# Two of x's row tiles on ScalarE's DMA queue and the remainder columns of w as fp32 on SyncE's, in a seven-product QKV projection

## The chip, the cores and the metric

The kernel runs on one core of one Trainium2 chip. The metric is the device time of one execution in microseconds (us). The engines are called as the profile calls them: PE is TensorE (PEld its weight loads), DVE is VectorE, ACT is ScalarE, POOL is GpSimd, SP is SyncE, which only issues DMAs here. ACTq and SPq are the DMA-issuing sides of ACT and SP.

## The reference

```python
batch, seq, hidden = 16, 512, 768
qkv = np.matmul(x, w_qkv)            # x: (16, 512, 768) fp32, w_qkv: (768, 2304) fp32
q, k, v = qkv[..., :768], qkv[..., 768:1536], qkv[..., 1536:]
return np.stack([q, k, v], axis=0).astype(np.float32)
```

So it is one matrix product of 8192 x 768 by 768 x 2304, whose columns are stored as three outputs.

## The kernel before, in words

**Tiling.** x's 8192 rows are 32 *pairs* of two 128-row tiles (`p` is a pair, `r` the tile in it). K = 768 is KT = 6 slices of 128, in two halves of KH = 3. w's 2304 columns are two column groups of 1024 (`q` = 0, 1, each two blocks `c` of CB = 512) and a remainder of REM = 256 columns between them (columns 1024 to 1279). A pair times a column group is a 2 x 2 by 2 x 2 block product, which `quad` and `do` (lines 233 to 289) make from seven products of three matmuls each instead of eight: products 1 and 2 use x and w rounded to bf16 (`xb`, `b1`), products 3 to 7 use sums of blocks of x (`sums_x`, line 211) and of w (`sum_w`, line 112; t1 to t4) and w's block `b22`. The remainder columns are plain bf16 matmuls of x's rounded tile with `w_rem` (`rem_row`, line 304, from `rem`; `rems_by_halves`, line 328). All matmuls of the seven products carry line 251, all those of `block` line 487, the remainder's lines 306 and 334.

**The first pairs.** At the start w is not there yet, so the first ND = 2 pairs (four row tiles) go another way. Their rows are loaded as they lie (`load_row`), cast to bf16 half by DVE and half by ACT (`cast_row`, lines 172 and 173), turned by PE against an identity (`turn_row`, line 190) and copied out of PSUM, and their products with the four 512-column blocks are plain bf16 matmuls in `block` (line 487), which takes the slices of w one after the other, in the order in which they land and are cast (`cast_j`, lines 463 and 465). Between the turns PE runs dummy matmuls on zeros (`busy`, line 458). From the third pair on, x is loaded in parts, turned by DVE (`transpose`, line 154), rounded by ACT or POOL (`round_row`, line 207, `round_x`) and summed.

**The order.** The schedule is written out by hand (`manual_schedule`): each engine runs its instructions in the order in which the program names them, and each DMA queue in the order of its issues. Eight completion semaphores are used in turn for the DMAs of SP and ACT, so that an issue waits for the landing of the eighth DMA before it. The start up to the third pair is in lines 428 to 590:

- SP issues the first row tile; ACT issues two *touches* (lines 431 and 432), 128 x 32 elements of w and of x that nobody reads, and then runs a tiny activation (line 433); SP issues the other three row tiles.
- SP issues 13 slices of w: column group 0, c = 0 (the first of its six K slices in two halves, `lo` and `hi`) and c = 1; then the third pair's rows in eight parts (`load_x_rows(2)`), then two blocks of column group 1 (`load_blocks(1, 0)`).
- POOL issues the remainder columns of w in two K halves, as DMAs that cast fp32 to bf16 (line 450). Two *holds*, one-element copies on POOL (line 445), keep these DMAs back until the last slice of c = 0 has landed, and later POOL work until the first part of the third pair's rows has.
- PE: eight dummies, the four tiles' turns with dummies between, `block(0, 0)` (27 matmuls, the first six of 256 columns), `block(0, 1)` (24), the remainder of the first two pairs by K halves (24, line 334), products 1 and 2 of the third pair (6), the third pair's remainder (12), and then the third pair's other products woven into `block(1, 0)`.
- ACT, behind `block(0, 1)`: the evacuations of tiles 0 and 1 (`late`, line 477), the rounding of the third pair's first tile, the first pair's remainder copy (line 323), tiles 2 and 3, the rounding of the second tile, the second remainder copy, the evacuation of product 1 (line 260).
- DVE: casts of w's slices, t1, one cast, t2, the third pair's two transposes, then its sums and t3, t4.

From the fourth pair on, `two`, `group` and `last` run the steady state.

Of the kernel before, what the change touches and what calls it, by code (L numbers as in the profile page):

```python
# [10 lines left out]
def kernel(  # L11
# [20 lines left out]
    nc = tc.nc  # L32
    P = 128
    G = 32
# [4 lines left out]
    KT = K // P  # L39
    KH = KT // 2  # L40
    KC = K // 4
    NP = M // (2 * P)
    CB = 512
    REM = N3 - 4 * CB
    Q_OFF = (0, 2 * CB + REM)
    R_OFF = 2 * CB
    fp32 = mybir.dt.float32
# [3 lines left out]
    add = mybir.AluOpType.add  # L51
    sub = mybir.AluOpType.subtract

    x_flat = x.rearrange("b t h -> (b t) h")
# [7 lines left out]
    o_pool = ctx.enter_context(tc.tile_pool(name="o", bufs=5))  # L62
# [7 lines left out]
    m_pool = ctx.enter_context(tc.tile_pool(name="m", bufs=2))  # L70
    ps_pool = ctx.enter_context(tc.tile_pool(name="ps", bufs=8, space=bass.MemoryType.PSUM))
# [5 lines left out]
    w_rem = [w_pool.tile([P, KH, REM], bf16, name="w_rem0"), None]  # L77
# [13 lines left out]
    def load_w(dst, j0, nj, off, cols):  # L91
        rows = w_qkv.rearrange("(p j) n -> p j n", j=KT)
        nc.sync.dma_start(dst, rows[:, j0:j0 + nj, off:off + cols])

    stage = {}

    def load_slices(c, cuts):
        t = tq_pool.tile([P, KT, CB], fp32, name="st0", tag="tq")
        stage[0, 0, c], stage[0, 1, c] = t[:, :KH, :], t[:, KH:, :]
        for j, nj, lo, hi in cuts:  # L100
            load_w(t[:, j:j + nj, lo:hi], j, nj, Q_OFF[0] + c * CB + lo, hi - lo)
# [10 lines left out]
    def sum_w(q, n):  # L112
        t1, t2, t3, t4 = ts[q]
        o, in0, in1 = {
            1: (t1, stage[q, 0, 1], stage[q, 0, 0]),
            2: (t2, stage[q, 1, 1], t1),
            3: (t3, stage[q, 1, 1], stage[q, 0, 1]),
            4: (t4, stage[q, 1, 0], t2),
        }[n]
        nc.vector.tensor_tensor(o, in0, in1, op=sub)  # L120

    xin, xf, xb, sr = {}, {}, {}, {}
# [8 lines left out]
    def load_x_rows(p, parts=range(8)):  # L131
        if p not in xin:
            xin[p] = xin_pool.tile([P, 2 * P // G, KC], fp32, name="xin")
        rows = x_flat[p * 2 * P:(p + 1) * 2 * P, :].rearrange("(g b) k -> b g k", b=G)
        for n in parts:
            r, i = divmod(n, 4)
            gs = slice(r * P // G, (r + 1) * P // G)
            nc.sync.dma_start(
                xin[p][i * G:(i + 1) * G, gs], rows[:, gs, i * KC:(i + 1) * KC]
            )  # L140
# [21 lines left out]

    def load_row(p, r):
        if r == 0:
            xin[p] = xin_pool.tile([P, 2, K], fp32, name="xin")
        row = (2 * p + r) * P
        nc.sync.dma_start(xin[p][:, r], x_flat[row:row + P, :])

    def copy_halves(dst, src):
        nc.vector.tensor_copy(out=dst[0], in_=src[0])
# [27 lines left out]
    act, dve = nc.scalar, nc.vector  # L200

    def round_row(p, r, eng):
        n = slice(r * P, (r + 1) * P)
        if r == 0:
            xb[p] = xb_pool.tile([P, KT, 2 * P], bf16, name="xb", tag="xb")
        if eng is act:
            eng.activation(xb[p][:, :, n], xf[p][:, :, n], ident)
        else:
            eng.tensor_copy(out=xb[p][:, :, n], in_=xf[p][:, :, n])
# [23 lines left out]
    def quad(p, q, pool=o_pool, tag="o"):  # L233
        u = Quad()
        u.p, u.q = p, q
        u.o = pool.tile([P, 2, 2 * CB], fp32, name="o", tag=tag)
        u.x = u.y = u.z = None
        return u

    def product(u, n, ps, start):  # L240
        t1, t2, t3, t4 = ts[u.q]
        if n <= 2:
            h = (n - 1) * KH
            lhs = [xb[u.p][:, h + j, :P] for j in range(KH)]
            rhs = [b1[u.q][:, h + j, :] for j in range(KH)]
        else:
            k, t = {3: (4, b22[u.q][:]), 4: (0, t4), 5: (1, t1), 6: (2, t2), 7: (3, t3)}[n]
            lhs = [sr[u.p][:, k, j, :] for j in range(KH)]
            rhs = [t[:, j, :] for j in range(KH)]
        for j in range(KH):  # L250
            nc.tensor.matmul(  # L251
                ps[:], lhs[j], rhs[j],
                start=(start and j == 0), stop=(j == KH - 1), skip_group_check=True,
            )

    def bank():
        return ps_pool.tile([P, CB], fp32, name="ps")

    def evacuate(u):
        nc.scalar.activation(u.o[:, 0, :CB], u.x[:], ident)  # L260

    def do(u, n, out=True):
        c11, c12 = u.o[:, 0, :CB], u.o[:, 0, CB:]
        c21, c22 = u.o[:, 1, :CB], u.o[:, 1, CB:]
        if n == 1:
            u.x = bank()
            product(u, 1, u.x, True)
            if out:
                evacuate(u)
        elif n == 2:  # L270
            u.z = bank()
            product(u, 2, u.z, True)
            nc.vector.tensor_tensor(c11, c11, u.z[:], op=add)  # L273
        elif n == 6:
            product(u, 6, u.x, False)
            nc.scalar.activation(c12, u.x[:], ident)  # L276
        elif n == 5:
            u.y = bank()
            product(u, 5, u.y, True)
        elif n == 7:  # L280
            product(u, 7, u.x, False)
            nc.scalar.activation(c22, u.x[:], ident)  # L282
            nc.vector.tensor_tensor(c22, c22, u.y[:], op=add)  # L283
        elif n == 4:
            product(u, 4, u.x, False)
            nc.scalar.activation(c21, u.x[:], ident)  # L286
        elif n == 3:
            product(u, 3, u.y, False)
            nc.vector.tensor_tensor(c12, c12, u.y[:], op=add)  # L289

    def rows_of(s, p, lo, hi):
        return out_flat[s, p * 2 * P:(p + 1) * 2 * P, lo:hi].rearrange("(r m) n -> m r n", m=P)
# [26 lines left out]
    def rem_copied(p, ps, eng=nc.sync):  # L319

        def copied():
            o = or_pool.tile([P, 2, REM], fp32, name="orem")
            act.activation(o[:], ps[:], ident)  # L323
            return lambda: eng.dma_start(rows_of(1, p, R_OFF - H, R_OFF - H + REM), o[:])

        return copied

    def rems_by_halves(pairs):
        banks = [ps_pool.tile([P, 2, REM], fp32, name="ps") for _ in pairs]
        for h in range(2):  # L330
            for p, ps in zip(pairs, banks):
                for r in range(2):
                    for j in range(KH):
                        nc.tensor.matmul(  # L334
                            ps[:, r, :], xb[p][:, h * KH + j, r * P:(r + 1) * P],
                            w_rem[h][:, j, :], start=(h == 0 and r == 0 and j == 0),
                            stop=(h == 1 and j == KH - 1), skip_group_check=True,
                        )
        return [rem_copied(p, ps) for p, ps in zip(pairs, banks)]

    def two(a, b, early, u=None, turns=()):

# [83 lines left out]
    ND = 2  # L426
    zero = xb_pool.tile([P, CB], bf16, name="zero", tag="xb")
    nc.vector.memset(zero[:], 0.0)
    load_row(0, 0)
    touch = m_pool.tile([P, 2, G], fp32, name="touch")  # L430
    nc.scalar.dma_start(touch[:, 0], w_qkv.rearrange("(p j) n -> p j n", j=KT)[:, 0, :G])  # L431
    nc.scalar.dma_start(touch[:, 1], x_flat[2 * P:3 * P, :G])
    nc.scalar.activation(tiny[:], zero[:, :1], ident)
    make_identity(nc, eye)
    load_row(0, 1)
    load_row(1, 0)
    load_row(1, 1)
    half = CB // 2
    load_slices(0, [(0, 1, 0, half), (0, 1, half, CB)] + [(j, 1, 0, CB) for j in range(1, KT)])
    load_slices(1, [(j, 1, 0, CB) for j in range(KT)])  # L440
    load_x_rows(2)

    def hold(src):
        mark = m_pool.tile([P, 1], fp32, name="mark")
        nc.gpsimd.tensor_copy(out=mark[:], in_=src)

    hold(stage[0, 1, 0][:, KH - 1, :1])
    for h in range(2):
        rows = w_qkv.rearrange("(p j) n -> p j n", j=KT)[:, h * KH:(h + 1) * KH]
        nc.gpsimd.dma_start(w_rem[h][:], rows[:, :, R_OFF:R_OFF + REM])  # L450
    hold(xin[2][:, 0, :1])
    load_blocks(1, 0)

    def busy(n):
# [94 lines left out]
    for f in late0:  # L549
# [3 lines left out]
    cast_j(0, 1, bt, 4, act)  # L553
    cast_j(0, 1, bt, 5, act)
    sum_w(0, 2)
    nc.gpsimd.tensor_copy(out=b22[0][:], in_=stage[0, 1, 1])
    late = block(
        0, 1, bt, [((j, ), range(4)) for j in range(KH)] + [(range(KH, KT), range(4))]
    )
    rems = rems_by_halves(range(2))  # L560
    transpose(2, 2)

    late[0]()
    late[1]()
    round_row(2, 0, act)
    rem_stores = [rems[0]()]
    late[2]()
    late[3]()
    round_row(2, 1, act)
    rem_stores.append(rems[1]())  # L570
    load_blocks(1, 1)
    for store in rem_stores:
        store()
    load_x_rows(3)
    for p in range(2):
        store_quad(quads[p, 0])
# [2 lines left out]
    sums[0](nc.gpsimd)  # L579
    sums[1](dve)  # L580
    sums[2](dve)
    sum_w(0, 3)
    sums[3](dve)
    sums[4](dve)

    u = quad(2, 0)
    do(u, 1)
    do(u, 2)
    cast_j(1, 0, b1[1], 0)
    rem2 = rem(2)  # L590
    middle(u, (5, 6))
# [120 lines left out]
```

## Time and profile before

| what | value |
|---|---|
| runs | 359.88, 359.97, 360.47 us; median 359.97 us |
| the profiled execution | 360.26 us, its span 358.5 us |
| PE / DVE / ACT / POOL busy | 351.8 / 231.7 / 185.5 / 178.5 us |
| DMA | 107.73 MB, 301 GB/s over the span |
| issues at the start | SP's four row tiles from 0.74 us, 13 slices of w from 2.59, the third pair's rows from 11.17, the blocks of column group 1 from 16.98 |
| POOL's two DMAs of the remainder | issued from 12.22 us, 6.7 us from issue to landing (median) |

Times in the profile run from the span's start. A matmul's busy time overlaps the next one's, so the spacing of starts is what counts for PE. A row of the timeline gives start, length, engine, line, operation, output and inputs, how many were merged, and in brackets how long the engine had stood idle before it and what ended the idle time.

### The profile page before, as it was taken

How to read it: one execution, taken by the hardware profiler on the slowest of the kernel's cores; microseconds unless marked ns; L12 is line 12 of the kernel's file. 1: busy time of each engine (PE TensorE's matmuls, PEld its weight loads, DVE VectorE, ACT ScalarE, POOL GpSimd, SP SyncE). 2: the span in 40 equal slices, each digit the busy share in tenths (PEclk: the TensorE clock that was granted, in tenths of full speed). 3: DMA queues.
4: the chain of work that ended last, by engine and by line, in shares of the span. 5: the costliest groups of instructions: out<-in, count | busy, mean ns of one | idle time of the engine just before them, and what ended most of it. 6: DMA issues, size and time to landing. Idle time of an engine off the chain costs nothing.

```text
span 358.5 us, 5212 instructions
## 1 busy us (share of the span) xinstructions
PE 351.8 (98%) x1760; PEld 252.6 (70%) x1780; DVE 231.7 (65%) x245; ACT 185.5 (52%) x316; POOL 178.5 (50%) x187
## 2 busy tenths in 40 slices
PE   8999999999999999999999999999999999999995
PEld 4465577767768687786867768687776867768764
DVE  3789776878475675746676474676647577544643
ACT  5469644445545545454554545545454544545443
POOL 0223775582664717447372664717447371754420
PEclk9999999999999999999999999999999999999999
DMA  7998999999999898989989799898989989755767
GB/s 265 347 373 313 323 353 360 369 346 342 339 298 317 286 261 328 261 317 299 289 323 250 309 283 332 282 264 329 268 293 307 294 321 251 312 217 224 273 243 256
DMA packets 82106, 107.73 MB, mean 301 GB/s; under 512 B 5408, under 2 KB 62240, under 8 KB 82080
## 3 DMA queue, kind: packets, MB, share of 16 engines
q1 hardware_dynamic: 74288, 101.86, 86.1%
q10 hardware_dynamic: 6992, 5.15, 5.9%
q0 software_dynamic: 800, 0.39, 0.8%
q8 instruction: 14, 0.23, 0.3%
q14 instruction: 12, 0.10, 0.1%
HBM read 32.28 MB, written 75.50 MB: 301 GB/s over the span
## 4 chain that ended last, share of the span: by engine, by line
PE 93%; DMA 4%; ACT 1%; ACTq 1%; issue 0%
PE ps L251 78%; PE ps L306 11%; PE ps L487 4%; DMA st<-in_w_qkv_dram 3%; DMA touch<-in_x_dram 1%; PE ps L334 1%; ACT o L286 0%; ACTq L385 0%; ACT orem L399 0%; ACT both L463 0%; ACTq L431 0%; ACTq L401 0%; ACTq L399 0%
## 5 line engine op out<-in xcount | busy, mean ns | idle before, releaser
L251 PE MATMUL ps<-t,s 128*128 128x512 f32 x720 | 178.5, 396 | 0.0
L251 PEld LDWEIGHTS ps<-t,s 128*128 128x128 f32 x720 | 134.9, 188 | 29.8 <-ACT o L276 0.3
L154 DVE STREAM_TRANSPOSE xf<-xin 128x1536 f32<-128x1536 f32 (+1 forms) x33 | 91.2, 2767 | 2.5 <-DMA xin<-in_x_dram 2.5
L218 POOL TENSOR_TENSOR s<-xf 128x384 fp32r<-128x384 f32 x29 | 30.8, 1061 | 116.4 <-PE ps L251 115.0
L251 PE MATMUL ps<-b,xb 128*128 128x512 bf16 x342 | 81.7, 379 | 1.2
L283 DVE TENSOR_TENSOR o<-o,ps 128x512 f32<-128x512 f32 x58 | 39.7, 685 | 60.2 <-ACT o L282 60.2
L251 PEld LDWEIGHTS <-xb 128*128 128x128 bf16 x360 | 33.8, 98 | 36.9 <-issue 4.7
L273 DVE TENSOR_TENSOR o<-o,ps 128x512 f32<-128x512 f32 x60 | 39.0, 681 | 29.5 <-PE ps L251 22.4
L282 ACT ACTIVATE o<-ps 128x512 f32<-128x512 f32 x58 | 34.7, 598 | 44.2 <-PE ps L251 44.2
L276 ACT ACTIVATE o<-ps 128x512 f32<-128x512 f32 x60 | 36.0, 600 | 36.6 <-PE ps L251 34.0
L289 DVE TENSOR_TENSOR o<-o,ps 128x512 f32<-128x512 f32 x60 | 41.1, 687 | 20.7 <-PE ps L251 19.6
L260 ACT ACTIVATE o<-ps 128x512 f32<-128x512 f32 x60 | 35.7, 597 | 31.3 <-PE ps L251 18.3
L251 PE MATMUL ps<-b,s 128*128 128x512 f32 x180 | 50.4, 389 | 0.0
L198 POOL CAST xb<-xf 128x1536 bf16<-128x1536 f32 x28 | 41.0, 1464 | 16.7 <-DVE xf L154 16.7
L286 ACT ACTIVATE o<-ps 128x512 f32<-128x512 f32 x60 | 35.9, 598 | 24.3 <-PE ps L251 21.3
L306 PE MATMUL ps<-w_rem,xb 128*128 128x256 bf16 x360 | 44.6, 273 | 0.0
L306 PEld LDWEIGHTS <-xb 128*128 128x128 bf16 x360 | 34.9, 98 | 11.0 <-issue 1.1
L251 PEld LDWEIGHTS ps<-b,s 128*128 128x128 f32 x180 | 33.8, 188 | 7.1
L219 POOL TENSOR_TENSOR s<-s,xf 128x384 fp32r<-128x384 f32 x29 | 29.3, 1009 | 1.3
L220 POOL TENSOR_TENSOR s<-xf 128x384 fp32r<-128x384 f32 x29 | 29.3, 1009 | 0.0
L222 POOL TENSOR_TENSOR s<-xf,s 128x384 fp32r<-128x384 f32 x29 | 29.3, 1009 | 0.0
L323 ACT ACTIVATE orem<-ps 128x512 f32<-128x512 f32 x31 | 18.5, 597 | 20.7 <-PE ps L306 10.9
(47 smaller groups left out, 127.4 us busy)
## 6 DMA issues: line engine op xcount, KB each, us to landing
out_dram<-o SPq DMA_DIRECT2D x62, 768.0 KB, 4.5
xin<-in_x_dram SPq DMA_DIRECT2D x90, 192.0 KB, 6.5
out_dram<-o SPq DMA_DIRECT2D x65, 256.0 KB, 3.7
out_dram<-orem SPq DMA_DIRECT2D x31, 256.0 KB, 5.5
xin<-in_x_dram ACTq DMA_DIRECT2D x22, 192.0 KB, 6.9
st<-in_w_qkv_dram SPq DMA_DIRECT2D x11, 256.0 KB, 5.2
st<-in_w_qkv_dram SPq DMA_DIRECT2D x3, 768.0 KB, 10.0
xin<-in_x_dram SPq DMA_DIRECT2D x4, 384.0 KB, 4.5
```

What stands on the lines that cost most here:

```text
L154: lambda g=g: nc.vector.transpose(turned[:, g:g + n], rows[:, g:g + n])
L198: nc.gpsimd.tensor_copy(out=xb[p][:], in_=t[:])
L218: 1: lambda g: g.tensor_tensor(s[:, 1], a21, a22, op=add),
L251: nc.tensor.matmul(ps[:], lhs[j], rhs[j], start=(start and j == 0), stop=(j == KH - 1), skip_group_check=True,)
L260: nc.scalar.activation(u.o[:, 0, :CB], u.x[:], ident)
L273: nc.vector.tensor_tensor(c11, c11, u.z[:], op=add)
L276: nc.scalar.activation(c12, u.x[:], ident)
L282: nc.scalar.activation(c22, u.x[:], ident)
L283: nc.vector.tensor_tensor(c22, c22, u.y[:], op=add)
L286: nc.scalar.activation(c21, u.x[:], ident)
L289: nc.vector.tensor_tensor(c12, c12, u.y[:], op=add)
L306: nc.tensor.matmul(ps, xb[p][:, j, r * P:(r + 1) * P], w_rem[j // KH][:, j % KH, :], start=(j == 0), stop=(j == KT - 1), skip_group_check= ...
```

## The change

- The touch of x goes. ACT now issues the touch of w, x's second row tile and its fourth; SP issues the first and the third, and then w's slices.
- The two holds and POOL's two casting DMAs go. SP loads the remainder columns as fp32 into a buffer of the output pool, in two K halves: the first after w's slices, then the first four parts of the third pair's rows, the second half, the other four parts. POOL casts each half to bf16, ahead of its cast of `b22`.
- PE runs the first K half of the first two pairs' remainder (12 matmuls), then products 1 and 2 of the third pair (6), then the second K half (12). On ACT product 1's evacuation stands behind the evacuations of tiles 2 and 3, and both remainder copies behind the rounding of the third pair's second tile. DVE's addition of product 2 stands ahead of t3.

```diff
-    def load_row(p, r):
+    def load_row(p, r, eng=nc.sync):
...
-        nc.sync.dma_start(xin[p][:, r], x_flat[row:row + P, :])
+        eng.dma_start(xin[p][:, r], x_flat[row:row + P, :])
...
-    def rems_by_halves(pairs):
-        banks = [ps_pool.tile([P, 2, REM], fp32, name="ps") for _ in pairs]
-        for h in range(2):
-            for p, ps in zip(pairs, banks):
...
-        return [rem_copied(p, ps) for p, ps in zip(pairs, banks)]
+    def rems_half(pairs, banks, h):
+        for p, ps in zip(pairs, banks):
+            for r in range(2):
+                for j in range(KH):
+                    nc.tensor.matmul(
+                        ps[:, r, :], xb[p][:, h * KH + j, r * P:(r + 1) * P],
+                        w_rem[h][:, j, :], start=(h == 0 and r == 0 and j == 0),
+                        stop=(h == 1 and j == KH - 1), skip_group_check=True,
+                    )
...
-    load_row(0, 0)
-    touch = m_pool.tile([P, 2, G], fp32, name="touch")
-    nc.scalar.dma_start(touch[:, 0], w_qkv.rearrange("(p j) n -> p j n", j=KT)[:, 0, :G])
-    nc.scalar.dma_start(touch[:, 1], x_flat[2 * P:3 * P, :G])
+    touch = m_pool.tile([P, G], fp32, name="touch")
+    nc.scalar.dma_start(touch[:], w_qkv.rearrange("(p j) n -> p j n", j=KT)[:, 0, :G])
+    for p in range(2):
+        load_row(p, 0)
+        load_row(p, 1, nc.scalar)
     nc.scalar.activation(tiny[:], zero[:, :1], ident)
     make_identity(nc, eye)
-    load_row(0, 1)
-    load_row(1, 0)
-    load_row(1, 1)
     half = CB // 2
     load_slices(0, [(0, 1, 0, half), (0, 1, half, CB)] + [(j, 1, 0, CB) for j in range(1, KT)])
     load_slices(1, [(j, 1, 0, CB) for j in range(KT)])
-    load_x_rows(2)
-
-    def hold(src):
-        mark = m_pool.tile([P, 1], fp32, name="mark")
-        nc.gpsimd.tensor_copy(out=mark[:], in_=src)
-
-    hold(stage[0, 1, 0][:, KH - 1, :1])
-    for h in range(2):
-        rows = w_qkv.rearrange("(p j) n -> p j n", j=KT)[:, h * KH:(h + 1) * KH]
-        nc.gpsimd.dma_start(w_rem[h][:], rows[:, :, R_OFF:R_OFF + REM])
-    hold(xin[2][:, 0, :1])
+    st_rem = o_pool.tile([P, KT, REM], fp32, name="str", tag="o")
+    load_w(st_rem[:, :KH], 0, KH, R_OFF, REM)
+    load_x_rows(2, range(4))
+    load_w(st_rem[:, KH:], KH, KH, R_OFF, REM)
+    load_x_rows(2, range(4, 8))
     load_blocks(1, 0)
...
     sum_w(0, 2)
+    for h in range(2):
+        nc.gpsimd.tensor_copy(out=w_rem[h][:], in_=st_rem[:, h * KH:(h + 1) * KH])
     nc.gpsimd.tensor_copy(out=b22[0][:], in_=stage[0, 1, 1])
     late = block(
         0, 1, bt, [((j, ), range(4)) for j in range(KH)] + [(range(KH, KT), range(4))]
     )
-    rems = rems_by_halves(range(2))
+    banks = [ps_pool.tile([P, 2, REM], fp32, name="ps") for _ in range(ND)]
+    rems_half(range(ND), banks, 0)
     transpose(2, 2)
 
     late[0]()
     late[1]()
     round_row(2, 0, act)
-    rem_stores = [rems[0]()]
+    u = quad(2, 0)
+    u.x, u.z = bank(), bank()
+    for n, ps in ((1, u.x), (2, u.z)):
+        product(u, n, ps, True)
+    rems_half(range(ND), banks, 1)
     late[2]()
     late[3]()
+    evacuate(u)
     round_row(2, 1, act)
-    rem_stores.append(rems[1]())
     load_blocks(1, 1)
-    for store in rem_stores:
-        store()
+    for p, ps in enumerate(banks):
+        rem_copied(p, ps)()()
     load_x_rows(3)
...
     sums[2](dve)
+    c11 = u.o[:, 0, :CB]
+    dve.tensor_tensor(c11, c11, u.z[:], op=add)
     sum_w(0, 3)
...
-    u = quad(2, 0)
-    do(u, 1)
-    do(u, 2)
     cast_j(1, 0, b1[1], 0)
```

More of the change, by code (lines that the diff above doesn't have):

```diff
@@ L326, in rem_copied @@
         return copied
-    def rems_by_halves(pairs):
-        banks = [ps_pool.tile([P, 2, REM], fp32, name="ps") for _ in pairs]
-        for h in range(2):
-            for p, ps in zip(pairs, banks):
[L332 to L338, printed above, removed]
-        return [rem_copied(p, ps) for p, ps in zip(pairs, banks)]
+    def rems_half(pairs, banks, h):
[7 more added lines that the diff above has]
+                    )
     def two(a, b, early, u=None, turns=()):
```

## The prediction

> **What bounds the kernel now.** First the page: busy time by engine, then its chain of work.
>
> ```profile
> PE 351.8 (98%) x1760; PEld 252.6 (70%) x1780; DVE 231.7 (65%) x245; ACT 185.5 (52%) x316; POOL 178.5 (50%) x187
> ...
> PE 93%; DMA 4%; ACT 1%; ACTq 1%; issue 0%
> ```
>
> TensorE is busy nearly always, and the chain that ended last is 93% TensorE. So only the rest of the chain can be saved. Where does it lie? The chain in order of time (start, length, what):
>
> ```profile
> 5.23 5.24 DMA st<-in_w_qkv_dram
> 10.48 6.09 DMA st<-in_w_qkv_dram
> 16.60 0.64 ACT both L463
> 17.28 2.32 PE ps L487 x10
> 19.60 2.62 PE ps L334 x24
> ```
>
> From 17.28 us to the last evacuations it is TensorE without a hole worth naming; before that it runs through w's slices. But the chain does not say how long TensorE stood still. `block` (L487) starts at 8.83; its 27 matmuls of q=0, c=0 (start to start 6 of 256 columns take 0.109 each, as the 24 in 2.62 above, and 21 of 512 take 0.2155) make 5.18, and the next 24 begin at 14.03: no stall. These 24 need 5.17, so the remainder (L334) could begin at 19.20; it begins at 19.43 (shown in the last fence below). **The last slice therefore costs 0.23 us**, not the six that its chain piece shows. What else can move is the start at 8.83, and the timeline shows what sets it (start, length, engine, line, operation):
>
> ```profile
> 5.29 1.06 PE L458 MATMUL ps<-zero 128*128 128x512 bf16 x2
> 6.49 0.84 PE L190 MATMUL ps<-eye,xc 128*128 128x128 bf16 x6
> 7.13 0.64 PE L458 MATMUL ps<-zero 128*128 128x512 bf16 x2
> 7.60 0.50 PE L190 MATMUL ps<-eye,xc 128*128 128x128 bf16 x6
> ...
> 8.46 0.54 PE L190 MATMUL ps<-eye,xc 128*128 128x128 bf16 x6
> 8.83 1.03 PE L487 MATMUL ps<-b,xb 128*128 128x256 bf16 x7
> ```
> ```profile
> 6.72 0.52 ACT L173 ACTIVATE xc<-xin 128x384 bf16<-128x384 f32 x1 [0.29 <-DMA xin<-in_x_dram]
> ...
> 7.88 0.52 ACT L173 ACTIVATE xc<-xin 128x384 bf16<-128x384 f32 x1
> ```
>
> x's fourth tile (issued 2.12, landed 5.7 later) is cast at 7.88 and turned at 8.46, and `block` follows. From issue plus time to landing, the four tiles land at 4.04, 5.1, 6.65 and 7.82, and w's first half slice at 2.59 + 5.6 = 8.19, close behind. By windows the DMA moved 124 GB/s in 1.5 to 2.5 us, 297 in 5.5 to 7, 383 in 7 to 8.5 and 402 in 8.5 to 13.5: from 2.5 us on it is full, and bytes decide. Later:
>
> ```profile
> 13.50:15.00 1.50, 1.50 (x9) 0.69 (x7) 1.25 (x3) 1.42 (x3) 0.42 (x1) 1.00 1.05 395
> 15.00:19.00 4.00, 3.93 (x19) 1.66 (x17) 3.23 (x4) 2.98 (x6) 0.26 (x2) 1.00 1.28 248
> ```
>
> (The last two columns are DMA share and GB/s.) While POOL's casting load of the remainder columns runs, the rate falls to 248. Under it the third pair's rows come in:
>
> ```profile
> 18.71 1.60 DVE L154 STREAM_TRANSPOSE xf<-xin 128x768 f32<-128x768 f32 x1 [0.25 <-DMA xin<-in_x_dram]
> 19.43 2.78 PE L334 MATMUL ps<-w_rem,xb 128*128 128x256 bf16 x24
> 20.35 0.84 ACT L207 ACTIVATE xb<-xf 128x768 bf16<-128x768 f32 x1 [1.41 <-DVE xf L154]
> 22.05 1.46 PE L251 MATMUL ps<-b,xb 128*128 128x512 bf16 x5
> ```
>
> Rounded rows are ready at 21.19 and wanted at 22.05, 0.86 of slack, which the change spends: it puts half of the 24 remainder matmuls (12 x 0.109 = 1.31) behind the third pair's first two products. With that order, today's times would bring product 1 at 22.05 - 1.31 = **20.74**. That is the mark I compare with.
>
> **The change part by part.**
>
> *x's tiles on two queues.* SP issues two tiles instead of four, so w's slices are issued some 0.95 earlier (two issues of about 0.43, and gaps); ACT issues touch, tile 2, tile 4. How two queues share the engines is seen in the touches, 16 KB each on ACT's queue: the first took 3.5 us (landed 4.24, beside tile 1 at 4.04), the second 4.0 (5.2, beside tile 2 at 5.1). A queue's packet seems to go in turn with one of the other queue's, as many packets each. Then tile 2 comes only after the touch, that is after tile 1, in turn with tile 3, and tile 4 in turn with w's first half slice. Tile 1 stays at 4.04; tiles 2 and 3 land together near tile 3's old 6.65, or 0.4 sooner if tile 3 follows as closely as tile 2 followed tile 1 (1.1); tile 4 waits for the half slice's 128 KB beside it, 0.34 us at 383 GB/s: 8.16. I take +0.3 for the start of `block`. Bounds: -0.4, if two queues lift 297 to 402 GB/s in 5.5 to 7 us (1.5 x 105/402); +1.5, under the second rival. The value is nearest to the half slice's own landing, 8.19, on which `block` hangs anyway. The Trainium skill, DMA: Bandwidth & Descriptors, section "Queues, rings and completion order", states this turn-taking, packet by packet, and its "Issuing engines are not separate DMA queues" that a second issuing engine only saves issue time; by that alone the start would gain nothing, and the touches' landings agree. ACT's third issue (0.43) delays its table load (1.28, from 1.66) and the tiny activation to about 3.6; the first cast at 4.08 hides it.
>
> *The second touch, the two holds and POOL's loads go.* No engine on the path waited for them. With w's slices alone on the queue the last one needs 4.74 MB moved. Summed over half-microsecond windows before, that is reached at 14.8; with the lag of about 1.0 that the others show it lands at 15.8 instead of 16.6, cast by 16.5. TensorE, started at 9.13, wants it at 9.13 + 5.20 + 14 x 0.2155 = 17.35. So **-0.23**, certain unless the start comes 0.9 earlier.
>
> *The remainder as fp32 between the rows.* SP's queue now holds 0.39 MB of w, four row parts (0.39), 0.39 of w, four parts. At 350 GB/s (between 333 in 19 to 21 us and 395) they land near 16.9, 18.0, 19.1 and 20.3. POOL casts each half: 0.73, half of its 128x1536 cast (1.47), up to the 2.20 that its 128x768 cast took beside VectorE. Ready by 19.1 and 21.3; wanted at 19.50 (9.13 + 5.20 + 5.17) and 19.50 + 2.61 = 22.1: **0**, covered by 0.4 and 0.8; uncovered up to 0.5. POOL's b22 cast (1.47 to 3.02) queues behind them and ends by 24.3; product 3 wants it near 27.7.
>
> *Product 1 earlier.* Rows at 18.0, VectorE free of t2's sum (1.76, from 16.2) at 18.0, transpose 1.60, round 0.84 and two hand-overs: 20.55. TensorE comes at 8.83 + 0.3 + 5.20 + 5.17 + 1.31 = 20.81. **0**; if the rows land at 18.7 as today, 21.2 and +0.4; at 19.2, +0.9.
>
> *Moved behind.* On ACT the evacuation of product 1 comes after the last two tiles' evacuations, near 22.4; VectorE's new addition waits for it and has sums until 23.2: 0. Both remainder copies stand behind round_row, ending near 24.3 (24.39 before); SP's stores wait for them, with eight loads of the fourth pair behind: unchanged. The two blocks of w behind the rows land earlier.
>
> **Sum:** 20.81 - 20.74 = **+0.07 us** (+0.30 - 0.23). From there TensorE's work is the same. The profiled execution took 360.26 (span 358.5, 1.76 around it): 360.33. It lay 0.29 over the median of the runs, 359.97, so I name 360.0.
>
> **The rivals.**
>
> *The start is filled (faster).* The DMA's poor stretches are 1.5 to 2.5 us (124 GB/s) and 5.5 to 7 (297, share 0.89). Two queues could keep the engines fed: against 402 they lost 0.28 and 0.16 MB, 1.1 us. Then TensorE reaches product 1 at 20.81 - 0.30 - 1.1 = 19.41 and the rows are ready at 20.55 - 1.1 = 19.45, so -1.3: 358.7 by the median. Against it: in the first stretch the packets wait though two tiles are already issued. Chance 0.11.
>
> *TensorE starts at half rate (slower).* Its 512-column matmuls start 0.427 apart until about 7.3 (the two at 5.29 take 1.06, the two at 7.13 only 0.64), 0.2155 apart from 9.7. It stands still at 6.15 to 6.49 only, since tile 2 is there at 5.1. If tile 2 lands at 6.65, cast 0.52, turning starts at 7.2: a hole of 1.0. If such a hole keeps the rate low, transposes (0.64), two dummies (0.85), transposes, a dummy (0.43), transposes follow from 7.2: 0.64 + 0.85 + 0.64 + 0.43 + 0.64 = 3.2, `block` at 10.4 instead of 8.83. That is +1.55 - 0.23 and a few slow matmuls, about +1.5: 361.5 by the median. It decides when tiles 2 and 3 land after about 6.4. The Trainium skill, TensorE: Matmul & The Clock Gate, "Part 1: The HAM clock gate", has this as a rule: half rate until a window of about 3.4 us has been busy. The rows' one switch near 7.3 agrees; whether a 1.0 us hole undoes it no row shows. Chance 0.19.
>
> *The third pair's rows come late (slower or the same).* w's half stands ahead of them, and they are asked for 1.31 earlier. Landing at 18.7 to 19.2 gives +0.4 to +0.9: 360.4 to 360.9. Against it: the 248 GB/s stretch goes. Chance 0.14, half of it over 0.2%.
>
> **How the numbers follow.** A measurement of this kernel tells about 0.2%, 0.7 us, from no change. Forecast 0.56, with 359.6 to 360.5 of its own. Faster 0.11 (first rival), slower 0.19 + 0.07 = 0.26, the same 0.63. The range, 359.4 to 361.3, leaves out most of the first rival and half of the second.
>
> **What would show it.** `block` starts near 9.1 (7.8 and 10.4 under the rivals); the casts of tiles 2 and 3 start one after the other near 6 to 6.6; no hole in the second 24 matmuls; L334's successor in two groups of 12 with six products between, the first of them at 20.8; DMA over 330 GB/s in 15 to 19 us. It is wrong if tile 4 lands before 7.5, or if TensorE stands before either half of the remainder.

## The result and the profile after

The changed kernel takes 361.96 us (median; 360.96 to 363.56), the kernel before in the same comparison 359.98 us: a ratio of 1.0052, 95% interval 1.0039 to 1.0065. It is **slower by 0.5%**, some 2.0 us, above the range of the prediction. The profiled execution took 362.22 us, its span 360.4 (before 360.26 and 358.5).

The page after, busy time and then the chain of work:

```profile
PE 351.8 (98%) x1760; PEld 252.3 (70%) x1780; DVE 231.5 (64%) x245; ACT 185.9 (52%) x316; POOL 177.2 (49%) x185
...
PE 91%; DMA 5%; ACT 1%; ACTq 1%; issue 1%; DVE 0%; SPq 0%; DVEq 0%
```

TensorE does exactly the work of before, 351.8 us; its share of the chain fell from 93% to 91% and DMA's rose from 4% to 5%. So what was added is waiting. The chain in order of time names it (start, length, what):

```profile
8.75 5.90 DMA st<-in_w_qkv_dram
...
14.66 5.32 DMA xin<-in_x_dram
...
20.11 1.56 DVE xf L154
...
21.69 0.85 ACT xb L207
...
22.59 0.39 PE ps L251
```

Before, w's last slice and then TensorE carried this stretch; now it is a part of the third pair's rows, its transposition and its rounding, and product 1 (L251) comes at 22.59 instead of the mark of 20.74. The timeline of the same kernel (start, length, engine, line, operation; in brackets the idle time before and what ended it):

```profile
9.07 5.35 PE L476 MATMUL ps<-b,xb 128*128 128x256 bf16 x26
...
17.13 0.63 ACT L452 ACTIVATE both<-st 128x512 bf16<-128x512 f32 x1 [0.41 <-DMA st<-in_w_qkv_dram]
...
19.97 1.47 PE L332 MATMUL ps<-w_rem,xb 128*128 128x256 bf16 x12
20.11 1.55 DVE L154 STREAM_TRANSPOSE xf<-xin 128x768 f32<-128x768 f32 x1 [1.11 <-DMA xin<-in_x_dram]
...
21.69 0.84 ACT L207 ACTIVATE xb<-xf 128x768 bf16<-128x768 f32 x1 [2.22 <-DVE xf L154]
...
22.25 1.60 DVE L154 STREAM_TRANSPOSE xf<-xin 128x768 f32<-128x768 f32 x1 [0.60 <-DMA xin<-in_x_dram]
...
22.59 1.47 PE L251 MATMUL ps<-b,xb 128*128 128x512 bf16 x5 [1.15 <-ACT xb L207]
```

`block` starts at 9.07, as forecast. The last slice is cast at 17.13 (16.60 before), so the remainder (L332) begins at 19.97 and not at 19.43. VectorE, free since 19.00, waits until 20.11 for the first tile's rows, and the remainder's half is over 1.30 before product 1 can begin. The queue's side of it, by windows (start:end; length; busy time of PE, PEld, DVE, ACT, POOL with counts; clock; DMA share; GB/s):

```profile
15.00:17.00 2.00, 2.00 (x10) 0.79 (x9) 2.00 (x3) 1.50 (x3) 0.00 (x0) 1.00 1.08 328
17.00:19.00 2.00, 1.79 (x9) 0.77 (x8) 1.86 (x2) 1.35 (x3) 0.40 (x1) 1.00 0.99 267
19.00:21.00 2.00, 2.00 (x16) 1.32 (x14) 0.89 (x1) 0.47 (x1) 0.68 (x1) 1.00 0.64 163
21.00:23.00 2.00, 0.83 (x6) 0.36 (x5) 1.40 (x2) 1.31 (x3) 1.58 (x2) 1.00 0.72 157
```

The rate at 15 to 19 us is 298 GB/s on average, not over 330, and then it falls to 163 and 157. The kernel before in the last two stretches:

```profile
19.00:21.00 2.00, 2.00 (x18) 1.60 (x17) 1.31 (x1) 0.65 (x1) 1.33 (x1) 1.00 1.11 333
21.00:23.00 2.00, 1.95 (x16) 1.42 (x15) 1.73 (x2) 1.59 (x4) 0.10 (x1) 1.00 1.02 391
```

### The profile page after: what moved, and what is told of

It reads as the page before. It is cut to its first block, busy times and chain, and to the rows that moved or that the text cites. A ratio compares the mean times of both kernels' runs of the same rounds, so it can differ in the third digit from the quotient of the medians.

```text
span 360.4 us, 5207 instructions
## 1 busy us (share of the span) xinstructions
PE 351.8 (98%) x1760; PEld 252.3 (70%) x1780; DVE 231.5 (64%) x245; ACT 185.9 (52%) x316; POOL 177.2 (49%) x185
## 3 DMA queue, kind: packets, MB, share of 16 engines
HBM read 32.26 MB, written 75.50 MB: 299 GB/s over the span
## 4 chain that ended last, share of the span: by engine, by line
PE 91%; DMA 5%; ACT 1%; ACTq 1%; issue 1%; DVE 0%; SPq 0%; DVEq 0%
PE ps L251 78%; PE ps L306 11%; DMA xin<-in_x_dram 3%; PE ps L476 3%; DMA st<-in_w_qkv_dram 2%; DVE xf L154 0%; PE ps L332 0%; ACT o L286 0%; ACTq L382 0%; ACT xb L207 0%; ACT orem L396 0%; SPq L93 0%; ACTq L169 0%; ACTq L427 0%; ACTq L398 0%
## 5 line engine op out<-in xcount | busy, mean ns | idle before, releaser
L251 PE MATMUL ps<-t,s 128*128 128x512 f32 x720 | 178.6, 396 | 0.0
L251 PEld LDWEIGHTS ps<-t,s 128*128 128x128 f32 x720 | 134.9, 188 | 29.8 <-ACT o L276 0.3
L251 PE MATMUL ps<-b,xb 128*128 128x512 bf16 x342 | 82.0, 379 | 2.3 <-ACT xb L207 1.1
L251 PEld LDWEIGHTS <-xb 128*128 128x128 bf16 x360 | 33.7, 98 | 38.3 <-issue 4.7
L260 ACT ACTIVATE o<-ps 128x512 f32<-128x512 f32 x60 | 35.8, 597 | 31.0 <-PE ps L251 19.1
L251 PE MATMUL ps<-b,s 128*128 128x512 f32 x180 | 50.5, 389 | 0.0
L198 POOL CAST xb<-xf 128x1536 bf16<-128x1536 f32 x28 | 40.9, 1462 | 17.5 <-DVE xf L154 17.5
L306 PE MATMUL ps<-w_rem,xb 128*128 128x256 bf16 x360 | 44.6, 273 | 0.0
L306 PEld LDWEIGHTS <-xb 128*128 128x128 bf16 x360 | 34.9, 98 | 10.8 <-issue 0.8
L251 PEld LDWEIGHTS ps<-b,s 128*128 128x128 f32 x180 | 33.8, 188 | 7.1
```

Of the source, the lines that this page charges most:

```text
L198: nc.gpsimd.tensor_copy(out=xb[p][:], in_=t[:])
L251: nc.tensor.matmul(ps[:], lhs[j], rhs[j], start=(start and j == 0), stop=(j == KH - 1), skip_group_check=True,)
L306: nc.tensor.matmul(ps, xb[p][:, j, r * P:(r + 1) * P], w_rem[j // KH][:, j % KH, :], start=(j == 0), stop=(j == KT - 1), skip_group_check= ...
```

## The experiments

Eight other kernels ran beside the changed one, and it and the kernel before were each profiled once more. **One table holds the reading of their profiles**, by the prediction's own terms: how much later than before `block` starts (8.83); how much longer it takes from there to the remainder (10.60 before; 10.37 without a stall); what product 1 waits beyond the matmuls that stand ahead of it; and what is lost between product 1 and the fourth pair's first remainder matmul. Each is a difference of starts in the timelines of one execution; their sum stands beside the difference of the two profiled executions' times. The kernel before, profiled again, shows how far such terms go without any change.

| kernel | start | last slice | product 1 waits | behind it | sum | profiled | ratio of times, interval |
|---|---|---|---|---|---|---|---|
| forecast | +0.30 | -0.23 | 0 | 0 | +0.07 | | |
| before_again (before) | -0.26 | 0.00 | 0 | 0.00 | -0.25 | +0.03 | one execution |
| changed | +0.25 | +0.31 | 1.30 | 0.00 | +1.86 | +1.96 | 1.0052 [1.0039, 1.0065] |
| after_again (the same) | -0.09 | -0.23 | 1.17 | 0.62 | +1.47 | +1.49 | one execution |
| x_only | -0.49 | +0.65 | 0 | 0 | +0.16 | +0.38 | 0.9996 [0.9985, 1.0007] |
| rem_only | +0.20 | -0.23 | 0.82 | 1.01 | +1.80 | +2.19 | 1.0046 [1.0029, 1.0063] |
| pool_kept | 0.00 | +0.07 | 0.73 | 0.01 | +0.81 | +0.96 | 1.0036 [1.0017, 1.0054] |
| order_undone | +1.51 | +0.09 | 0 | 0.29 | +1.89 | +1.99 | 1.0065 [1.0047, 1.0082] |
| rows_ahead | +1.35 | +0.70 for both | | 0.00 | +2.05 | +2.79 | 1.0086 [1.0065, 1.0107] |
| no_w | -0.45 | +0.95 | 1.42 | -0.02 | +1.90 | +1.95 | 1.005 [1.0032, 1.0068] |
| no_w_held | -0.50 | +0.77 | 0.15 | 0.02 | +0.44 | +0.48 | 1.0001 [0.9991, 1.0011] |
| parts4 | -0.23 | -0.24 | 2.37 | 1.65 | +3.55 | +4.01 | 1.0114 [1.0094, 1.0134] |

(In rows_ahead products 1 and 2 stand ahead of the whole remainder, so that its last slice and its wait for rows stand in one term. In order_undone and rows_ahead TensorE runs at half clock until 10.98 and 11.48 us, into `block`: that makes 0.30 and 0.63 of what stands under the last slice.)

**The two parts of the change, each alone.** x_only has the four row tiles on two queues and otherwise the kernel before; rem_only has the rest and x's loads as before.

```diff
 x_only, against before:
-    nc.scalar.dma_start(touch[:, 1], x_flat[2 * P:3 * P, :G])
...
+    for p in range(2):
+        load_row(p, 0)
+        load_row(p, 1, nc.scalar)
...
 rem_only, against the changed kernel:
-        load_row(p, 1, nc.scalar)
...
+    load_row(0, 1)
+    load_row(1, 0)
+    load_row(1, 1)
```

> Only the x part of the change: tiles 2 and 4 on ACT's queue, the touch of x gone; the remainder still cast by POOL's DMAs, the old order of products. Theory A (the loss is the third pair's rows landing late behind w's half, because SP may have only eight DMAs under way and one slow DMA engine holds them all): block starts 0.25 us later, the 24 matmuls of c=1 still meet the last slice, product 1 keeps its slack, so +0.1 to +0.3 us. Theory B (the tiles on ACT hold up SP's issues of w's slices, as tile 4's landing releases the first slice of c=1, and everything behind is late): the slices of c=1 land 0.7 to 1.0 us later than before here too, and the kernel loses 0.8 us or more.

> Only the remainder part: fp32 on SP's queue by K halves between the third pair's rows, products 1 and 2 between the halves; x's tiles and both touches as before. Theory A: block starts at 8.83 as before, the rows still land at 19.5 to 20, so product 1 waits and the loss is +1.2 to +1.8 us. Theory B: without the x part the slices land as before or 0.7 us earlier, the rows near 18.5, product 1 near 21.0, and the loss is 0.4 us at most.

x_only ran at 0.9996 [0.9985, 1.0007], rem_only at 1.0046 [1.0029, 1.0063]: the whole loss is in the remainder part. The table also says what became of x's part. In x_only `block` started 0.49 earlier, and the last slice of w came 0.65 later against it: the slices did not come any sooner than before (16.7 us, before 16.6), and a start ahead of them only waits longer. So theory B had the late slices, but not its loss. In rem_only the first tile's rows were transposed at 19.02, earlier than theory A had them, and the second tile's only at 22.86.

**The same two kernels profiled again.**

> The changed kernel once more, for a second profile. If the slow packets of w's slices at 10 to 11 us and the engine that falls 2 us behind belong to the change, they are there again and the rows land near 20.1. If they are chance (theory C), this profile has them elsewhere, and the rows land within 17.5 to 19.

> The kernel before once more, for a second profile. If the slow packets at 5.4 to 6.3 us belong to the fourth tile's first reads, they are there again; if they are chance, they are elsewhere. The rows landed at 18.7 and the last slice at 16.6; by theory C these move by up to 1 us while the time stays, since product 1 has 0.86 us of slack.

Before took 360.29 us again, the changed kernel 361.75. Its last slice landed at 15.6 this time (forecast 15.8) and TensorE ran through the slices without a stall, as forecast; product 1 still waited 1.17, and 0.62 went behind it. So the wait for the rows does not come from the late slice of the first profile. Theory C is not settled by it: the rows were transposed at 19.10, at the edge of its 17.5 to 19.

**The loads of w taken away.** no_w has no load of the remainder columns; POOL writes zeros into `w_rem` where it would cast.

```diff
-    load_w(st_rem[:, :KH], 0, KH, R_OFF, REM)
-    load_x_rows(2, range(4))
-    load_w(st_rem[:, KH:], KH, KH, R_OFF, REM)
-    load_x_rows(2, range(4, 8))
+    load_x_rows(2)
...
-        nc.gpsimd.tensor_copy(out=w_rem[h][:], in_=st_rem[:, h * KH:(h + 1) * KH])
+        nc.gpsimd.memset(w_rem[h][:], 0.0)
```

> The changed kernel without any load of the remainder columns: POOL fills w_rem with zeros where it cast before, so the 256 remainder columns are not computed. Theory A (the rows are late because 0.79 MB of w stands between w's slices and them): the rows' two halves land near 17.3 and 18.5, product 1 waits for nothing, and the time is 0.1 to 0.4 us under the kernel before. Theory E (the rows are late from a DMA engine that lags anyway, or from the eight-in-flight limit on small parts): they land at 18.5 or later and product 1 still waits 0.5 us or more, time +0.4 to +1.

The time stayed, 1.005 [1.0032, 1.0068], which seemed to acquit the loads. But the kernel had changed something else. In the changed kernel POOL's `b22` cast stands behind its casts of the two halves and starts at 22.19. With nothing to wait for, it started at 17.19, beside VectorE's t2, which took 3.06 us instead of 1.76, and the transposition began at 20.19 with no wait for a DMA at all (the rows had landed between 17.2 and 19.1). This run decides nothing; no_w_held, below, does.

**The order put back.** order_undone keeps the loads and puts products 1 and 2 behind all 24 remainder matmuls.

```diff
+    rems_half(range(ND), banks, 1)
...
-    rems_half(range(ND), banks, 1)
```

> The changed kernel with products 1 and 2 of the third pair behind all 24 remainder matmuls, as before the change; loads as in the change. Theory A (data late): TensorE waits for the second half of the remainder instead, cast near 21.5 to 22.3 and wanted at 20.5, and then for the sums, so the loss stays, +1.2 to +1.8 us. Theory D (the new order spends the rows' slack, and that is the loss): product 1 is wanted 1.31 later and the loss falls to 0.5 us or less.

It is no better, 1.0065 [1.0047, 1.0082]. Product 1 waits for nothing, but the *second* tile's rows are late as well. Its timeline, and the same rows of the kernel before:

```profile
22.66 1.58 DVE L154 STREAM_TRANSPOSE xf<-xin 128x768 f32<-128x768 f32 x1 [1.57 <-DMA xin<-in_x_dram]
...
24.49 0.60 ACT L260 ACTIVATE o<-ps 128x512 f32<-128x512 f32 x1 [1.54 <-PE ps L251]
...
24.98 0.83 ACT L207 ACTIVATE xb<-xf 128x768 bf16<-128x768 f32 x1
```
```profile
21.17 1.57 DVE L154 STREAM_TRANSPOSE xf<-xin 128x768 f32<-128x768 f32 x1 [0.85 <-DMA xin<-in_x_dram]
...
23.05 0.86 ACT L207 ACTIVATE xb<-xf 128x768 bf16<-128x768 f32 x1
23.35 1.47 PE L306 MATMUL ps<-w_rem,xb 128*128 128x256 bf16 x12
```

Before, the second tile was rounded at 23.91 and wanted in the middle of L306, at 23.35 + 0.66 = 24.01: a slack of 0.10. In order_undone its transposition began 1.50 later, and it was rounded at 25.81, 1.90 later; the other 0.4 is ScalarE's, which first evacuated product 1 (L260), and that was put back by a start at half rate (`block` at 10.34, see below). Without it the second tile could be rounded near 25.1 (22.66 + 1.58 + 0.84, an estimate), 1.1 after it was wanted before: that much its rows would cost, whatever the order of the products. The time of this profiled execution, 362.25, is also that of the ones with mean clocks of 0.999 or 1.0 (362.14 to 363.17). These had no start at half rate to lose by; the estimate gives them 1.1 of their 2.0 us or more, and the rest is not shown.

**The loads put back.** pool_kept has the holds and POOL's casting loads of before, and the new order.

```diff
-    st_rem = o_pool.tile([P, KT, REM], fp32, name="str", tag="o")
-    load_w(st_rem[:, :KH], 0, KH, R_OFF, REM)
...
+    load_x_rows(2)
...
+    hold(stage[0, 1, 0][:, KH - 1, :1])
+    for h in range(2):
+        rows = w_qkv.rearrange("(p j) n -> p j n", j=KT)[:, h * KH:(h + 1) * KH]
+        nc.gpsimd.dma_start(w_rem[h][:], rows[:, :, R_OFF:R_OFF + REM])
+    hold(xin[2][:, 0, :1])
```

> The changed kernel with the remainder cast by POOL's DMAs behind the two holds, as before; the new order of products and x's two queues stay. Theory A: the rows come as in the kernel before, rounded near 21.2 to 21.6, product 1 wanted near 20.5 to 20.7, so +0.4 to +0.9 us from the order alone, and no later wait. Theory D: nearly the whole loss, +1.2 us or more.

1.0036 [1.0017, 1.0054], between the two theories: **the new order alone costs** (with x's part, which cost nothing by itself) 1.1 us by the medians and 1.3 by the ratio. The executions spread from 360.28 to 364.24, two of the twelve with mean clocks of 0.995 and 0.99. In its profile, at full clock, the loss is one wait, 0.73 at product 1: the first tile's rows come as in x_only (transposition at 19.02; 19.19 there), they are wanted 1.31 earlier, and the slack was 0.86 in the kernel before. Behind product 1 nothing is lost, since the second tile is transposed at 21.51.

**The rows ahead of w.** rows_ahead loads all eight row parts first, then both halves of w, and runs products 1 and 2 ahead of the whole remainder.

```diff
+    load_x_rows(2)
     load_w(st_rem[:, :KH], 0, KH, R_OFF, REM)
-    load_x_rows(2, range(4))
     load_w(st_rem[:, KH:], KH, KH, R_OFF, REM)
-    load_x_rows(2, range(4, 8))
...
-    rems_half(range(ND), banks, 0)
...
-    rems_half(range(ND), banks, 1)
+    for h in range(2):
+        rems_half(range(ND), banks, h)
```

> The changed kernel with all eight parts of the rows ahead of both halves of the remainder, and products 1 and 2 ahead of all 24 remainder matmuls. Theory A: the rows land near 17.5 and 18.7, product 1 starts near 20.2 instead of 21.6 to 22.6 and the sums are no later than in the kernel before; TensorE idles 0.7 to 1.0 us ahead of product 1 and nowhere behind it: +0.4 to +0.8 us over the kernel before. Theory E: rows at 18.5 or later, +1.2 us or more.

The worst so far, 1.0086 [1.0065, 1.0107]: theory E's time, without its late rows. They did come earlier (transposition at 18.86, with no wait for a DMA), and product 1, at 21.47, waited only 0.28 behind the slices. In this profile the loss is the start at half clock (1.35, and 0.63 in `block`), and 0.67 us that come far behind the table's terms, where a later pair's rows were late for VectorE, and its addition for TensorE:

```profile
81.88 2.97 DVE L154 STREAM_TRANSPOSE xf<-xin 128x1536 f32<-128x1536 f32 x1 [2.69 <-DMA xin<-in_x_dram]
...
85.47 0.81 PE L251 MATMUL ps<-b,xb 128*128 128x512 bf16 x3 [0.46 <-DVE o L273]
```

In the kernel before, that transposition waited 0.99. Four of the six executions have mean clocks of 0.999 or 1.0 and took 362.35 to 364.17 all the same. No profile shows one of these, so what this order costs them stays open.

**The loads taken away, with POOL held back.** no_w_held writes the zeros at the start and holds POOL's `b22` cast behind the rows, so that POOL is out of VectorE's way.

```diff
-    st_rem = o_pool.tile([P, KT, REM], fp32, name="str", tag="o")
...
+    for h in range(2):
+        nc.gpsimd.memset(w_rem[h][:], 0.0)
+    load_x_rows(2)
...
+    nc.gpsimd.tensor_copy(out=mark[:], in_=xin[2][:, 4, :1])
```

> The changed kernel without the loads and casts of w's last 256 columns: w_rem is zeroed by POOL at the start, so the remainder columns are not computed; a one-column copy on POOL holds the b22 cast behind the first row parts, as in the changed kernel. Theory 'the halves of w stand in front of the rows in SyncE's queue' (0.79 MB, 2.6 us of all DMA engines): without them the rows land near 17.5 and 18.7 us, product 1 waits for nothing, and the time is 360.0 to 360.3 (-0.2 to +0.3 against before). Rival 'the rows are late whatever stands in front, because the engines lag behind the last slice of w': still 360.7 or more, with product 1 waiting 0.5 or more.

The loss is gone: 1.0001 [0.9991, 1.0011], in the range of the first theory. Its timeline:

```profile
18.64 3.04 DVE L154 STREAM_TRANSPOSE xf<-xin 128x768 f32<-128x768 f32 x2
...
20.25 0.84 ACT L207 ACTIVATE xb<-xf 128x768 bf16<-128x768 f32 x1 [1.06 <-DVE xf L154]
...
21.15 1.47 PE L251 MATMUL ps<-b,xb 128*128 128x512 bf16 x5
```

Both tiles are transposed in one go (x2, no DMA in brackets), and product 1 follows the remainder's half with 0.15 of wait, in the new order. Here, too, one slice of w was late (0.77 in the table), and product 1 hardly waited, so a late slice alone doesn't bring the loss. With this order it takes loads of these columns ahead of the rows in their queue, or (pool_kept, the smaller loss) beside them. And with no load of these columns at all the kernel is just as fast as before: in this order, taking the loads off the queue altogether wins nothing.

**Fewer, larger parts.** parts4 loads the third pair's rows as four DMAs of 192 KB between the two halves of w, instead of eight of 96 KB.

```diff
-    load_x_rows(2, range(4))
+    load_x(2, nc.sync)
     load_w(st_rem[:, KH:], KH, KH, R_OFF, REM)
-    load_x_rows(2, range(4, 8))
```

> The changed kernel with the third pair's rows as 4 DMAs of 192 KB, for both tiles between the two halves of w, instead of 8 of 98 KB around the second half. Theory 'starvation': the many small DMAs leave the engines without work (82 and 37 GB/s at 20.5 to 21.5 us in the changed kernel), so with four DMAs less the first rows land by 19.3, and the time is 360.5 to 361.0 (+0.5 to +1.0). Theory 'time of the bytes': the first tile's rows now share the engines with the second tile's, are ready near 21.8, product 1 waits as long or longer, and the time is 361.3 to 362.0 (+1.3 to +2.0).

1.0114 [1.0094, 1.0134], **outside both**. From 20 us on the DMA engines did not starve any more, but the first tile's rows, sharing the engines with the second's, were there at 20.1, and TensorE stood still from 20.43 to 22.64. Its windows:

```profile
20.00:21.00 1.00, 0.43 (x4) 0.14 (x2) 0.83 (x1) 0.00 (x0) 0.11 (x1) 1.00 1.12 427
21.00:22.00 1.00, 0.00 (x0) 0.00 (x0) 1.00 (x2) 0.26 (x1) 1.00 (x2) 1.00 0.98 381
22.00:23.00 1.00, 0.36 (x1) 0.21 (x3) 1.00 (x1) 1.00 (x3) 1.00 (x1) 1.00 1.05 397
23.00:24.00 1.00, 0.95 (x5) 0.39 (x4) 0.86 (x3) 1.00 (x4) 0.79 (x2) 0.94 1.05 408
24.00:25.00 1.00, 1.00 (x6) 0.75 (x5) 1.00 (x2) 0.83 (x2) 0.21 (x1) 0.50 1.04 406
...
27.00:28.00 1.00, 1.00 (x9) 0.87 (x8) 1.00 (x3) 0.92 (x2) 0.00 (x0) 0.86 1.03 382
```

Of the wait, the "time of the bytes" had the direction and most of the size (rows ready near 21.8 there, rounded at 22.58 here); "starvation" had neither. Neither had what follows: the granted clock (third column from the end) is 0.50 from about 23.9 to 27.3, and the 1.65 us behind product 1 in the table are matmuls at half rate. Half clock for 3.4 of 362 us lowers the mean by 0.005; five of the six executions have mean clocks of 0.993 to 0.995, the sixth 0.997, so five of them, at least, probably paid it.

## Why the prediction was wrong, point by point

- **x's tiles on two queues: +0.3. Right** for this execution (+0.25, through the steps given: tiles 2 and 3 cast one behind the other from 6.59, TensorE idle 0.97 before their turns), but that is luck: six other profiles of such a start lie between -0.50 and 0.00, two, at half rate, at +1.35 and +1.51, and the unchanged start came at -0.26 and +0.20 (before_again, rem_only). That the tiles come in turn is what the Trainium skill says ("DMA: Bandwidth & Descriptors", Queues, rings and completion order: each engine takes a packet from each queue that has work, in turn), and the trace agrees: tile 3 on SP's queue and tile 2 on ACT's landed at 6.38 and 6.56. That no time came of it has the reason shown by x_only: w's slices set the time behind it.
- **Last slice: -0.23.** It was so in after_again, rem_only and parts4; in the first profile it was +0.31, and x_only, no_w_held and no_w lost 0.65, 0.77 and 0.95. I called it certain, from sums of bytes, and the slice's landing varies by over a microsecond (15.6 and 17.1 in the two profiles of the changed kernel).
- **"The remainder as fp32 between the rows" is the step that failed.** I let the four loads land near 16.9, 18.0, 19.1 and 20.3 at 350 GB/s: 2.2 us from the last slice's landing to that of the first tile's rows, 4.5 to the second's. By the landings in the traces it took 2.9 to 3.4 and 5.0 to 6.8 us (the changed kernel, after_again, rem_only, order_undone): 230 to 270 GB/s for the first 0.79 MB. And the third rival had against it that "the 248 GB/s stretch goes". That row was misread. The page's queues before (packets, MB, share of 16 engines):

```profile
q0 software_dynamic: 800, 0.39, 0.8%
...
HBM read 32.28 MB, written 75.50 MB: 301 GB/s over the span
```

  The casting DMA is counted by the bf16 bytes that it writes: 0.39 MB for 0.79 MB read. With the other 0.39 MB, 15 to 19 us of before read up to (248 x 4 us + 390 KB) / 4 us = 345 GB/s, an estimate that puts the whole load into this stretch (741 of its 768 packets of data start there). There was no stretch at 248 GB/s to be rid of. HBM reads after are the same, 32.26 MB. Nor is the casting load dear in time of the engines: 0.8% of 358.5 is 2.9 us of all sixteen (768 packets at 61 ns), and the same columns in SP's queue take 768 packets of 1 KB at 53 to 60 ns on average in the same four traces, 2.6 to 2.9 us.
  What changed is where this time stands: before, beside the rows, as a second queue; now ahead of them in the same one. The transpositions of the two tiles began at 18.4 to 19.2 and 21.0 to 21.5 in the four profiles with casting loads (before, before_again, x_only, pool_kept), at 19.0 to 20.1 and 22.3 to 22.9 in the four with fp32 loads ahead of them. So the second tile's rows are late in all four, the first's by less, and not beyond the spread in each. POOL's casts were priced rightly: in the changed kernel they took 1.08 and 0.83 us, and TensorE waited for neither half.
- **"Product 1 earlier": 0**, if the rows land at 18.0. By my own conditional (+0.4 for 18.7, +0.9 for 19.2) pool_kept's 0.73 at 19.02 is right. So the step's rule held, and its input did not. The order spent 1.31 of a slack of 0.86, and the loads, put ahead of the same rows, wanted that slack a second time.
- **"Moved behind": 0 was wrong where the second tile is late.** It had 0.10 of slack before, and I gave its landing (20.3) without asking when it was wanted. It cost 1.01 in rem_only, 0.62 in after_again, and nothing in the first profile, where product 1 had already waited 1.30.
- **The rivals.** "The third pair's rows come late" was the right mechanism, at a chance of 0.14 and a price of 0.4 to 0.9; it costs 1.3 to 1.8. "The start is filled" was half true: in the changed kernel the windows from 5 to 8 us show 379 to 404 GB/s, where 5.5 to 7 had 297 before, and nothing came of it. "TensorE starts at half rate" happened in some executions only, in the profiles of order_undone and rows_ahead; the clock of all nine executions of the changed kernel is 0.999 or 1.0, so it is not its loss. The hole of 1.0 that the rival asked for came (6.20 to 7.17), and the clock stayed at 1.0. order_undone, by windows:

```profile
5.00:6.00 1.00, 0.45 (x3) 0.00 (x0) 0.24 (x1) 0.49 (x1) 0.00 (x0) 1.00 1.01 386
6.00:7.00 1.00, 0.00 (x0) 0.00 (x0) 0.27 (x1) 0.27 (x1) 0.00 (x0) 1.00 1.04 391
7.00:8.00 1.00, 0.69 (x7) 0.63 (x8) 0.64 (x3) 0.67 (x2) 0.00 (x0) 0.78 1.05 405
8.00:9.00 1.00, 1.00 (x6) 0.52 (x5) 0.42 (x2) 0.90 (x2) 0.00 (x0) 0.50 1.06 408
9.00:10.00 1.00, 1.00 (x9) 0.73 (x7) 0.76 (x3) 0.48 (x1) 0.00 (x0) 0.50 1.05 408
```

  TensorE idle for 1.9 us, then half clock, `block` at 10.34: the rival's 10.4.

**What stays open.** In the changed kernel the queue also ran dry (163 and 157 GB/s). SP's last three row parts and the next block of w were issued at 17.12, 18.57, 19.10 and 19.57, each 0.02 us after the landing of the eighth DMA before it, so that small parts left little in flight. parts4 shows that with four DMAs fewer the rate holds from 20 us on, but as its rows come together it can't say what the dry stretch costs by itself. And why in some executions one slice of w lands a microsecond late was not tried. The traces show how: a DMA raises its semaphore 16 times, and in the changed kernel's first profile the last slice had 15 of them at 15.64 and the sixteenth at 17.11, the fourth row part 18.70 and 19.98. In after_again these pairs are 15.47 and 15.61, 18.73 and 18.98. So one share in 16 was late in the first profile, and made its rows about a microsecond later than they were in after_again; product 1 waited in both.

## What to carry to other kernels

A casting DMA is counted by what it writes: before a window with a low rate is taken for idle bandwidth, hold it against the bytes that HBM read and the engines' time. When a change asks for data earlier and also puts bytes ahead of them in their queue, both are paid from the same slack; work that slack out for every tile that lands there, the second as well as the first. And an experiment that removes a load also removes what waited for it: look for what now runs earlier, and beside what.

## What the runs showed of the hardware

- A hole of TensorE of 2.2 us (parts4) was followed, 1.2 us after work came back, by 3.4 us at half clock; holes of 1.9 us (order_undone, rows_ahead) by the same, 0.3 and 0.6 us after. Holes of 1.2 and 1.0 us (the changed kernel) and of 1.4 (after_again) were followed by none. The Trainium skill ("TensorE: Matmul & The Clock Gate", Part 1: The HAM clock gate) describes a free-running window of about 3.4 us by which the clock is halved or freed. The length of the slow stretch agrees with it; but a hole need not fill such a window to be paid for.
- VectorE's 128x1536 fp32 sum took 3.06 us beside POOL's 128x1536 cast to bf16 (no_w) and 1.76 without it (no_w_held).
- A casting DMA is counted by what it writes: 0.39 MB for 0.79 MB read (before, against the 32.28 and 32.26 MB of HBM reads before and after).
- In 15 to 19 us the kernel before read up to 345 GB/s (the estimate above) with the casting loads beside SP's queue; with the same columns in SP's queue 283 to 307 were read (order_undone, after_again, the changed kernel, rem_only). How much of the difference is the second queue's, no run separates.
